# Applying the chunk inverses once per unit instead of once per chunk in an RWKV-7 recurrence

## The chip, the cores and the metric

The kernel runs on one core of a Trainium2 chip. The metric is the device time of one execution in microseconds (us). Before the change the median of three timed runs is 1398.25 us (1395.99 to 1398.87).

TensorE (PE in the profile) multiplies and writes its results to PSUM, the accumulation memory; its weight loads are listed apart as PEld. VectorE (DVE), ScalarE (ACT) and GpSimd (POOL) work element by element, and SyncE (SP) issues most DMAs.

## The reference

One layer for a prompt of 1024 tokens and 8 samples of 4 tokens: an RWKV-7 recurrence beside dilated attention, then a gated merge, an output projection and a layer norm. The change touches the recurrence of the prompt, cut here to its core (per head, with a 64 x 64 state S):

```python
def step(S, inp):
    r_t, w_t, k_t, v_t, kk_t, a_t = inp
    sa = jnp.einsum('bhvk,bhk->bhv', S, -kk_t)
    S = (S * w_t[:, :, None, :] + sa[..., None] * (kk_t * a_t)[:, :, None, :]
         + v_t[..., None] * k_t[:, :, None, :])
    return S, jnp.einsum('bhvk,bhk->bhv', S, r_t)

S_fin, o = lax.scan(step, wkv0.astype(F32), xs)
```

Each token reads the state that all tokens before it have written, so the plain form has 1024 steps in a row.

## The kernel before

**Chunks.** The 1024 tokens are cut into 16 chunks of 64. Inside a chunk the tokens' effect on each other is a lower triangular matrix, and the corrections `sa` of all its tokens come from one triangular solve. Two heads (e = 0, 1) share the 128 partitions. A *unit* is a pair of heads and half of the sequence, so 8 chunks; there are 8 units (4 pairs, 2 halves), numbered 0 to 7 here.

**What a unit prepares** (`unit`, L304): the decays `E`, the tile `KR` with the kappa vectors in its middle columns and the receptance vectors in its outer ones, the tile `BK`, and `AT`, which is `BK` times `KR` per chunk and head (L369) under a mask (L376, VectorE). From `AT` and the values in `W` comes `R0`, the tokens' own part of the right-hand side (L415, copied by L419). The inverse of the triangular part is made by `inverse` (L425): 32 x 32 blocks go out to DRAM, 31 steps on VectorE (L440, L443) solve them, and they come back.

**What a unit's recurrence does** (`scan`, L454): first the blocks are joined to 64 x 64 inverses with two batches of small matmuls (L466, copied by L472, then L476, copied by L482 back into `AT`). Then for each chunk in turn:
- L495: `KR` of the chunk times the state. One half of the rows is kappa times the state, the other half the receptance times the state.
- L497 (VectorE): the first half plus `R0` gives `R`; L498 (ScalarE) copies the other half to the output tile `Ot`.
- L502: the chunk's inverse times `R`, two matmuls, one a head. L503 (ScalarE) copies it negated into `W`.
- L507: `BT` (the transposed `BK`) times `W` is the update; L510 (VectorE) adds it to the decayed state `SD`, which L493 (ScalarE) has scaled.

After the eighth chunk L518 makes the rest of the output in one batch, and `norm` (L527) normalises it (its transposes on TensorE are L547, copied by L549).

**What sets the order.** TensorE's order is written out by hand: `run_streams` (L700) keeps a clock, and each generator (recurrence, norms, inverses, preparations) yields how long its piece takes TensorE and after how long its next piece is due. Whoever is due goes first, the recurrence ahead of the others; when nobody is due, one piece of a projection follows (L171, a third of a bank's 12 matmuls, four matmuls). The projections are the input matrix's columns for the recurrence, its gates and the rest, and they fill the stage until none is left. ScalarE, VectorE and the DMA queues are ordered by the scheduler. PSUM is shared out by tags: projections "pj" (four banks), the recurrence "sc" (two), the preparations and norms "g" (two). A tile of a tag waits until an earlier one of that tag has been read. The tag "t" is a ring of six buffers in SBUF.

Of the kernel before, what the change touches and what calls it, by code (L numbers as in the profile page):

```python
# [14 lines left out]
AF = mybir.ActivationFunctionType  # L15
ALU = mybir.AluOpType
AX = mybir.AxisListType

P = 128
# [13 lines left out]
D_PM, D_HOP, D_ST, D_GN, D_IN, D_WU = 0.53, 0.99, 1.54, 12.6, 11.0, 0.48  # L33
# [49 lines left out]
def tile_layer(ctx: ExitStack, tc: tile.TileContext, A: dict, O: list):  # L83
    nc = tc.nc
    V, S, G, T, SP = nc.vector, nc.scalar, nc.gpsimd, nc.tensor, nc.sync
# [10 lines left out]
    def mk(pool, shape, tag, bufs=None, dt=F32):  # L96
        uid[0] += 1
        return pool.tile(list(shape), dt, tag=tag, name=f"{tag}_{uid[0]}", bufs=bufs)

    def ps(tag, cols=512, parts=P):  # L100
        pool = pspool if tag == "pj" else pp[0]
        return mk(pool, [parts, cols], tag, {"pj": PJ, "sc": 2, "g": 6 - PJ, "s": 1, "t": 2, "o": 1}[tag])


    ident = mk(cpool, [P, P], "ident")[:]
# [9 lines left out]
    rp = rw_stack.enter_context(tc.tile_pool(name="rp", bufs=1))  # L115
# [94 lines left out]
    for c in range(3):  # L210
# [5 lines left out]
        if c == 2:  # L216
            prm = mk(cpool, [P, 57], "prm")
            b = ps("g")
# [10 lines left out]
    b = ps("g")  # L229
# [224 lines left out]
    def scan(j, hf, KR, AT, W, BT, R0, E, bon, st, Xd, blk, out):  # L454

        T1 = mk(rp, [P, 8, 32], "T1", 1)
        quads = [(p, 64 * (1 - p), n, n // 4, 2 * (n % 4) + p) for p in range(2) for n in range(8)]
        for p in range(2):
            u = 64 * (1 - p)
            for b in (1, 0):  # L460
                SP.dma_start(blk(p, b, slice(0, 2)), Xd[p, b].rearrange("e c j i -> j e c i"))
            V.transpose(T1[u : u + 32], AT[u : u + 32, :, p::2, u : u + 32])
        both = [quads[8 * p + n] for n in range(8) for p in range(2)]
        pm = ps("sc")
        for _, u, n, e, c in both:
            T.matmul(  # L466
                pm[u + 32 : u + 64, 32 * n : 32 * n + 32], AT[u : u + 32, e, c, u + 32 : u + 64], T1[u : u + 32, n, :],
                start=True, stop=True,
            )
        for p in range(2):  # L470
            u = 64 * (1 - p)
            S.activation(T1[u + 32 : u + 64], pm[u + 32 : u + 64, 0:256].rearrange("p (a b) -> p a b", a=8), AF.Copy, scale=-1.0)  # L472
        yield (0.5, D_PM)
        pg = ps("sc")
        for _, u, n, e, c in both:
            T.matmul(  # L476
                pg[u : u + 32, 32 * n : 32 * n + 32], T1[u + 32 : u + 64, n, :], AT[u + 32 : u + 64, e, c, u + 32 : u + 64],
                start=True, stop=True,
            )
        for p in range(2):  # L480
            u = 64 * (1 - p)
            S.activation(  # L482
                AT[u : u + 32, :, p::2, u + 32 : u + 64], pg[u : u + 32, 0:256].rearrange("p (a b c) -> p a b c", a=2, b=4), AF.Copy
            )
        yield (0.6, D_PM)

        Ot = mk(rp, [P, 4, P], "Ot", 2)
        for c in range(8):
            p, c2 = c % 2, c // 2
            u, v = slice(64 * (1 - p), 64 * (1 - p) + 64), slice(64 * p, 64 * p + 64)  # L490
            S0, S1 = st[c % 2], st[1 - c % 2]
            SD = mk(rp, [P, P], "SD", 1)
            S.activation(SD[:], S0[:], AF.Copy, scale=E[:, c, 64:65])  # L493
            pr = ps("sc")
            T.matmul(pr[:, 0:P], KR[:, c2, 2 * p : 2 * p + 2, :], S0[:], start=True, stop=True)  # L495
            R = mk(rp, [P, P], "R", 1)
            V.tensor_tensor(R[u], pr[u, 0:P], R0[u, c2, :], ALU.add)  # L497
            S.activation(Ot[v, c2, :], pr[v, 0:P], AF.Copy)  # L498
            yield (0.2, D_HOP)
            pu = ps("sc")  # L500
            for e in range(2):
                T.matmul(pu[u, 64 * e : 64 * e + 64], AT[u, e, c, u], R[u, 64 * e : 64 * e + 64], start=True, stop=True)  # L502
            S.activation(W[u, c, :], pu[u, 0:P], AF.Copy, scale=-1.0)  # L503
            yield 0.4, D_WU

            pS = ps("sc")
            T.matmul(pS[:, 0:P], BT[:, c, :], W[:, c, :], start=True, stop=True)  # L507
            for e in range(2):
                d = slice(64 * e, 64 * e + 64)
                V.scalar_tensor_tensor(S1[d, d], pS[d, d], E[d, c, 64:65], SD[d, d], ALU.mult, ALU.add)  # L510
            yield (0.2, D_ST)


        po = ps("g")
        for c in range(8):
            c2, v = c // 2, slice(64 * (c % 2), 64 * (c % 2) + 64)
            for e in range(2):
                T.matmul(  # L518
                    po[v, c2 * P + 64 * e : c2 * P + 64 * e + 64], AT[:, e, c, v], W[:, c, 64 * e : 64 * e + 64],
                    start=True, stop=True,  # L520
                )
        V.tensor_tensor(Ot[:], Ot[:], po.rearrange("p (a b) -> p a b", a=4), ALU.add)
        yield (2.0, 0.0)
        out.append((j, hf, Ot, bon))
# [156 lines left out]
    def scans():  # L681
        for u in range(8):
            while done["inv"] <= u or done["unit"] <= u:
                yield None
            args = ready[u]
            yield from scan(*args, *inv[u], looped)
            if args[1]:
                state_out(args[0], args[9])
                yield 0.1, 0.0
            done["scan"] += 1  # L690
# [59 lines left out]
    def rec_step(t, w):  # L750
        Ss, kv, vv, oo = (rec[n] for n in ("S", "kv", "vv", "oo"))
        part = slice(8 * w, 8 * w + 8)
        R = Ss[:, part, :]
        bc = lambda i: kv[:, t, i, :].unsqueeze(1).to_broadcast([P, 8, 64])
# [4 lines left out]
        sa = mk(sp, [P, 8], "sa", 2)  # L759
        yield V.tensor_tensor(tm[:], R, bc(1), ALU.mult)  # L760
        yield V.tensor_reduce(sa[:], tm[:], AX.X, ALU.add)
        yield V.tensor_tensor(R, R, bc(0), ALU.mult)
        yield V.tensor_tensor(tm[:], vb(sa[:]), bc(2), ALU.mult)
        yield V.tensor_tensor(R, R, tm[:], ALU.subtract)
        yield V.tensor_tensor(R, R, kvp[:], ALU.add)  # L765
# [429 lines left out]
    for h in range(4):  # L1195
# [5 lines left out]
        for g in range(3):  # L1201
# [11 lines left out]
            a, b_ = attend(h, g, z["q"], z["k"], z["v"], ml, os_), s_scores(h, g, Sa, sm)  # L1213
# [136 lines left out]
```

## Time and profile before

| | |
|---|---|
| median of the timed runs | 1398.25 us |
| the profiled execution, in all | 1401.51 us |
| its span on the core | 1399.7 us |
| mean granted TensorE clock | 0.992 of full speed |
| first and last L495 (state product of a chunk) | 151.0 and 596.4 us |
| last L518 (rest of the output) | 602.3 us |
| costliest line, L171 (projections) | three rows of 401.6, 382.9 and 384.4 us |

The page lists for each engine the busy time and its share of the span. In a row on a line of the kernel stand the line, the engine, the operation, the tiles written and read with their shapes, then the busy time, the mean of one in ns, and the idle time of the engine ahead of it with what ended it. TensorE runs a 32-bit matmul as two records, so L502's 128 instructions are 256 rows. A matmul's end is modelled and overlaps the next one's start.

### The profile page before, as it was taken

To read this page: it belongs to the slowest core of one execution; us is meant where nothing else is said; L and a number is where in the kernel's file an instruction comes from. 1 tells how busy PE (TensorE), PEld (TensorE's weight loads), DVE (VectorE), ACT (ScalarE), POOL (GpSimd) and SP (SyncE) were. 2 spreads that over 40 slices of the span, in tenths; PEclk is the share of its full clock that TensorE was granted. 3 is DMA by queue.
4 is the path that set the end of the run, shared out by engine and by line. 5 is a ranking of instruction groups with operands and counts; after the bars stand their busy time and mean duration, and the time that the engine had idled before them with its cause. 6 is when DMAs were issued, how large, how long until landed. Compare 5 with 4: busy or idle time off the path is not lost.

```text
span 1399.7 us, 25258 instructions
## 1 busy us (share of the span) xinstructions
PE 1354.1 (97%) x9765; PEld 1250.6 (89%) x9765; DVE 814.9 (58%) x2219; ACT 460.6 (33%) x1075; POOL 81.2 (6%) x92
## 2 busy tenths in 40 slices
PE   7999999999999999998999999999999999999997
PEld 7998988898888889998999889989998899898884
DVE  4358767587776767343655485547233524565675
ACT  4333444444344443321332323322323234132110
POOL 0000000000000000001000000000000000025122
PEclk9999999999999999999999999999999999999999
DMA  6112222312313233237545454545565556687121
GB/s 213 54 46 74 60 78 80 97 50 73 88 51 89 77 89 101 81 96 141 102 106 117 113 128 101 123 116 133 97 151 122 122 128 153 173 252 243 61 90 53
DMA packets 339743, 151.29 MB, mean 108 GB/s; under 512 B 188945, under 2 KB 329031, under 8 KB 339367
## 3 DMA queue, kind: packets, MB, share of 16 engines
q1 hardware_dynamic: 249190, 133.55, 35.1%
q10 hardware_dynamic: 90432, 16.13, 6.3%
q8 instruction: 77, 1.26, 0.4%
q14 instruction: 44, 0.35, 0.1%
HBM read 110.35 MB, written 38.97 MB: 107 GB/s over the span
## 4 chain that ended last, share of the span: by engine, by line
PE 74%; DVE 13%; DMA 7%; issue 2%; ACT 2%; SPq 1%; POOL 1%; DVEq 0%; ACTq 0%
PE pj L171 51%; PE pj L1310 7%; PE o L931 2%; PE s L894 2%; DVE X L443 2%; DVE tm L440 2%; DMA cb<-cd 2%; DMA gt<-gd 1%; PE t L914 1%; DMA kv<-vd 1%; PE sc L502 1%; PE s L1013 1%; PE g L369 1%; DVE wlo L162 1%; DVE st L510 1%
## 5 line engine op out<-in xcount | busy, mean ns | idle before, releaser
L171 PE MATMUL pj<-xhi,whi 128*128 128x352 f32 x1848 | 401.6, 338 | 4.8 <-ACT whi L161 3.7
L171 PE MATMUL pj<-xhi,wlo 128*128 128x352 f32 x1848 | 382.9, 329 | 4.7 <-DVE wlo L162 4.7
L171 PE MATMUL pj<-xlo,whi 128*128 128x352 f32 x1848 | 384.4, 329 | 0.0
L171 PEld LDWEIGHTS pj<-xhi,whi 128*128 128x128 f32 x1848 | 304.5, 190 | 21.7 <-issue 10.4
L171 PEld LDWEIGHTS pj<-xhi,wlo 128*128 128x128 f32 x1848 | 309.0, 190 | 8.1 <-DVE wlo L162 5.3
L171 PEld LDWEIGHTS pj<-xlo,whi 128*128 128x128 f32 x1848 | 308.7, 190 | 2.9 <-issue 0.6
L162 DVE TENSOR_TENSOR wlo<-wraw,whi 128x512 fp32r<-128x512 f32 x162 | 111.6, 690 | 83.2 <-ACT whi L161 82.4
L161 ACT ACTIVATE whi<-wraw 128x512 fp32r<-128x512 f32 x162 | 100.8, 626 | 128.3 <-PE pj L171 79.1
L904 ACT ACTIVATE Sm<-Sm,nm 128x128 f32<-128x128 f32 (+1 forms) x96 | 42.4, 443 | 70.5 <-DVE nm L901 70.5
L510 DVE SCALAR_TENSOR_TENSOR st<-sc,E,SD 64x64 f32<-64x64 f32 x128 | 36.2, 283 | 47.0 <-PE sc L507 45.5
L1310 PE MATMUL pj<-wl,mh 128*128 128x512 f32 (+1 forms) x144 | 56.8, 394 | 0.0
L440 DVE TENSOR_TENSOR tm<-Y,X 128x60 f32<-128x60 f32 (+24 forms) x248 | 52.6, 212 | 6.3
L443 DVE TENSOR_TENSOR X<-X,tm 128x60 f32<-128x60 f32 (+24 forms) x248 | 52.0, 210 | 6.4
L896 DVE CUSTOM_DVE_ANT_0 Sm<-s,cst 128x128 f32<-128x128 f32 (+1 forms) x96 | 29.6, 346 | 40.4 <-PE s L894 40.4
L493 ACT ACTIVATE SD<-st,E 128x128 f32<-128x128 f32 x64 | 25.7, 401 | 58.5 <-DVE st L510 58.5
L819 ACT ACTIVATE k<-pj 128x352 f32<-128x352 f32 (+1 forms) x36 | 16.3, 456 | 84.9 <-PE pj L171 79.9
L757 POOL TENSOR_TENSOR kvp<-vv,kv 128x512 f32<-128x512 f32 x16 | 20.0, 1252 | 353.0 <-DVE Ss L765 226.7
L819 ACT ACTIVATE q<-pj 128x352 f32<-128x352 f32 (+1 forms) x36 | 16.4, 456 | 70.5 <-PE pj L171 68.3
L931 PE MATMUL o<-PT,Vt 128*128 128x128 f32 x280 | 38.5, 275 | 0.0
L894 PE MATMUL s<-k,q 128*128 128x128 f32 (+1 forms) x192 | 37.6, 325 | 0.0
L931 PEld LDWEIGHTS o<-PT,Vt 128*128 128x128 f32 x280 | 36.5, 191 | 0.6 <-ACT o L936 0.4
L819 ACT ACTIVATE v<-pj 128x352 f32<-128x352 f32 (+1 forms) x36 | 16.1, 451 | 61.3 <-PE pj L171 61.0
(295 smaller groups left out, 1756.2 us busy)
## 6 DMA issues: line engine op xcount, KB each, us to landing
wraw<-in_w_in_dram SPq DMA_DIRECT2D x146, 256.0 KB
gd<-zt SPq DMA_DIRECT2D x48, 176.0 KB
gt<-gd SPq DMA_DIRECT2D x48, 176.0 KB
vs<-bt ACTq DMA_DIRECT2D x48, 128.0 KB
kc<-in_cache_kv_g_dram SPq DMA_DIRECT2D x48, 128.0 KB
Vt<-vs ACTq DMA_DIRECT2D x12, 512.0 KB
cb<-cd SPq DMA_DIRECT2D x12, 512.0 KB
zd<-zt SPq DMA_DIRECT2D x24, 176.0 KB
```

Source lines behind the costliest of these rows:

```text
L161: S.activation(hi[:], raw[:], AF.Copy)
L162: V.tensor_tensor(lo[:], raw[:], hi.bitcast(F32)[:], ALU.subtract)
L171: T.matmul(out, w[wi][:, n % 4, :], x[:, n % 4, :], start=first and n == 0, stop=last and n == 11)
L440: V.tensor_tensor(tm, Y[:, r : r + 1, r + 1 : 32].to_broadcast([P, m, n]), X[:, 0:m, r : r + 1].to_broadcast([P, m, n]), ALU.mult)
L443: V.tensor_tensor(X[:, 0:m, r + 1 : 32], X[:, 0:m, r + 1 : 32], tm, ALU.subtract)
L510: V.scalar_tensor_tensor(S1[d, d], pS[d, d], E[d, c, 64:65], SD[d, d], ALU.mult, ALU.add)
L819: S.activation(classes(dst[:], d)[:, :, t0 // d : (t0 + n) // d], b[:, 0:n].rearrange("p (i c) -> p c i", c=d), AF.Copy)
L894: T.matmul(r, qT[:, i * P : (i + 1) * P], kT[:, keys[i][0] * P : keys[i][0] * P + n], start=True, stop=True)
L896: V.tensor_tensor_reduce(out=Sm[:, i, 0:n], in0=r, in1=m3 if g == 2 else m12[:, 256 - n : 256], scale=1.0, scalar=NEG, op0=ALU.add, op1=AL ...
L904: S.activation(Sm[:, i, 0:n], Sm[:, i, 0:n], AF.Exp, scale=SCALE, bias=nm[:, x : x + 1], accum_out=ml[:, g, 1, i : i + 1])
L931: T.matmul(po[:, (i % 4) * P : (i % 4 + 1) * P], st["Vt"][:, kb_, :], PT[:, n * P : (n + 1) * P], start=m == 0, stop=m == len(keys[i]) - 1,)
L1310: T.matmul(pb[0:n, :], a[:, k, 0:n], wk, start=x == 0, stop=x == len(prods) - 1)
```

## The change

Applying the inverse is linear, so it can be done to the two parts of the right-hand side apart: to the kappa vectors and to `R0`. Neither needs the state, so both are done ahead of the loop for all eight chunks of the unit:

- four transposes on TensorE turn the kappa part of `KR` (L467 in the changed kernel), and two ScalarE copies (L471) put it into a new tile `kT` of the ring "t";
- after the blocks are joined (now L474, L480, L484, L490), 16 matmuls of 64 x 64 multiply each chunk's inverse with its kappa (L500), into two "sc" banks, and ScalarE writes them negated over the kappa columns of `KR` (L505);
- 16 more (L510) multiply the inverses with `R0`, and ScalarE writes that negated over `R0` (L514).

In the loop the state product (L525) then gives the solved correction directly. VectorE adds `R0` into `W` (L526), and the update (L531, L534) follows. L502, L503 and the tile `R` are gone, as is their due time.

```diff
@@ scan @@
+        pk = ps("sc")
+        for c2 in range(4):
+            T.transpose(pk[:, c2 * P : (c2 + 1) * P], KR[:, c2, 1:3, :], ident)
+        kT = mk(rp, [P, 4, P], "t", 6)
+        for p in range(2):
+            u, v = slice(64 * (1 - p), 64 * (1 - p) + 64), slice(64 * p, 64 * p + 64)
+            S.activation(kT[u], pk[v, :].rearrange("p (a b) -> p a b", a=4), AF.Copy)
         pm = ps("sc")
         for _, u, n, e, c in both:
...
         yield (0.6, D_PM)
 
+        chunks = [(c // 2, c % 2, e) for c2 in range(4) for e in range(2) for c in (2 * c2, 2 * c2 + 1)]
+        pk = [ps("sc") for p in range(2)]
+        for c2, p, e in chunks:
+            u = slice(64 * (1 - p), 64 * (1 - p) + 64)
+            T.matmul(
+                pk[p][64 * e : 64 * e + 64, 64 * c2 : 64 * c2 + 64],
+                kT[u, c2, 64 * e : 64 * e + 64], AT[u, e, 2 * c2 + p, u], start=True, stop=True,
+            )
+        for p in range(2):
+            S.activation(KR[:, :, 1 + p, :], pk[p][:, 0:256].rearrange("p (a b) -> p a b", a=4), AF.Copy, scale=-1.0)
+        yield (1.3, 0.0)
+        pu = ps("sc")
+        for c2, p, e in chunks:
+            u = slice(64 * (1 - p), 64 * (1 - p) + 64)
+            T.matmul(
+                pu[u, c2 * P + 64 * e : c2 * P + 64 * e + 64],
+                AT[u, e, 2 * c2 + p, u], R0[u, c2, 64 * e : 64 * e + 64], start=True, stop=True,
+            )
+        S.activation(R0[:], pu.rearrange("p (a b) -> p a b", a=4), AF.Copy, scale=-1.0)
+        yield (1.3, D_PM)
+
         Ot = mk(rp, [P, 4, P], "Ot", 2)
         for c in range(8):
...
             T.matmul(pr[:, 0:P], KR[:, c2, 2 * p : 2 * p + 2, :], S0[:], start=True, stop=True)
-            R = mk(rp, [P, P], "R", 1)
-            V.tensor_tensor(R[u], pr[u, 0:P], R0[u, c2, :], ALU.add)
+            V.tensor_tensor(W[u, c, :], pr[u, 0:P], R0[u, c2, :], ALU.add)
             S.activation(Ot[v, c2, :], pr[v, 0:P], AF.Copy)
             yield (0.2, D_HOP)
-            pu = ps("sc")
-            for e in range(2):
-                T.matmul(pu[u, 64 * e : 64 * e + 64], AT[u, e, c, u], R[u, 64 * e : 64 * e + 64], start=True, stop=True)
-            S.activation(W[u, c, :], pu[u, 0:P], AF.Copy, scale=-1.0)
-            yield 0.4, D_WU
 
             pS = ps("sc")
             T.matmul(pS[:, 0:P], BT[:, c, :], W[:, c, :], start=True, stop=True)
```

Three places of the order show it. First TensorE in one chunk of the loop of unit 0, before (from the state product L495 to the next one; "pj" are projection banks, "sc" the recurrence's):

```order
L495 MATMUL sc_1719<-st_80_482,KR_885 128x128
L171 MATMUL pj_1583<-xlo_10_88,whi_1682 128x352 x4
L171 MATMUL pj_1584<-xhi_8_86,whi_1682 128x352 x4
L502 MATMUL sc_1736<-R_1721,AT_976 64x64 x2
L171 MATMUL pj_1584<-xhi_8_86,wlo_1683 128x352 x4
L507 MATMUL sc_1744<-W_1017,BT_1029 128x128
```

The same engine and place in the changed kernel, where the state product is L525 and the update L531:

```order
L525 MATMUL sc_1721<-st_79_481,KR_885 128x128
L171 MATMUL pj_1582<-xhi_8_86,whi_1727 128x352 x4
L171 MATMUL pj_1582<-xhi_8_86,wlo_1728 128x352 x4
L531 MATMUL sc_1739<-W_1017,BT_1029 128x128
L171 MATMUL pj_1582<-xlo_10_88,whi_1727 128x352 x4
L171 MATMUL pj_1583<-xhi_8_86,whi_1727 128x352 x4
L171 MATMUL pj_1583<-xhi_8_86,wlo_1728 128x352 x4
L525 MATMUL sc_1760<-st_80_482,KR_885 128x128
```

The two small matmuls and the group of projections behind them have left the chunk: it has five groups of projections where it had six.

Second, TensorE at the start of the recurrence of unit 1, before: the two joining batches (L466, L476), with the second half of the next unit's masked products (L369, eight matmuls into two "g" banks) between them, then the last unit's output transposes (L547):

```order
L466 MATMUL sc_2370<-T_425_2363,AT_1345 32x32 x16
L369 MATMUL g_2389<-KR_2276,BK_2285 128x128
L369 MATMUL g_2390<-KR_2276,BK_2285 128x128
...
L476 MATMUL sc_2401<-AT_1345,T_425_2363 32x32 x16
L547 MATMUL g_2420<-ident_69,Ot_1668 128x128 x4
L388 MATMUL g_2432<-t_2288,cst_76 128x512
L495 MATMUL sc_2438<-st_79_481,KR_1230 128x128
```

The same place on TensorE in the changed kernel:

```order
L467 MATMUL sc_2350<-ident_69,KR_1230 128x128 x4
L474 MATMUL sc_2358<-T_412_2343,AT_1345 32x32 x16
L571 MATMUL g_2377<-ident_69,Ot_1718 128x128 x4
L369 MATMUL g_2388<-KR_2244,BK_2253 128x128
L369 MATMUL g_2389<-KR_2244,BK_2253 128x128
...
L484 MATMUL sc_2400<-AT_1345,T_412_2343 32x32 x16
L388 MATMUL g_2420<-t_2256,cst_76 128x512
L500 MATMUL sc_2423<-AT_1345,t_2355 64x64
...
L510 MATMUL sc_2443<-R_264_1501,AT_1345 64x64 x16
```

The output transposes (now L571) have come ahead of the masked products and take one of the two "g" banks there. In units 3 and 5 it is the same; in units 2, 4 and 6 both masked products, L571 and the transposes of `BK` (L406) are ahead of L467, with one projection group between the joining batches; in units 0 and 7 there is only that group.

Third, ScalarE at the start of unit 1, before:

```order
L472 ACTIVATE T_425_2363<-sc_2370 32x256 x2
L482 ACTIVATE AT_1345<-sc_2401 32x8x32 x2
L549 ACTIVATE Ot_1668<-g_2420,prm_339 128x512
L399 ACTIVATE W_2443<-g_2444 64x4x128
L498 ACTIVATE Ot_2435<-sc_2438 64x128
```

And in the changed kernel, where L471 copies `kT` and L505 the kappa columns of `KR`:

```order
L471 ACTIVATE t_2355<-sc_2350 64x512 x2
L480 ACTIVATE T_412_2343<-sc_2358 32x256 x2
L573 ACTIVATE Ot_1718<-g_2377,prm_339 128x512
L309 ACTIVATE t_2586<-m_798,prm_339 128x512
L490 ACTIVATE AT_1345<-sc_2400 32x8x32 x2
L505 ACTIVATE KR_1230<-sc_2423 128x4x64
L505 ACTIVATE KR_1230<-sc_2424 128x4x64
L514 ACTIVATE R_264_1501<-sc_2443 128x512
```

The two copies of `kT` stand ahead of those of the first joining batch (T1, printed as `T`), and the output's copy L573 behind both, ahead of the copies into `AT`. In unit 0 the next unit's Square (L309) stands between the copies of `kT` and of T1.

## The prediction

> **What bounds the kernel now.** I read the page first, then the table by stage, then the chain, then single instructions in order of time.
>
> ```profile
> span 1399.7 us, 25258 instructions
> PE 1354.1 (97%) x9765; PEld 1250.6 (89%) x9765; DVE 814.9 (58%) x2219; ACT 460.6 (33%) x1075; POOL 81.2 (6%) x92
> ...
> 250.00:350.00 100.00, 97.21 (x852) 87.96 (x848) 74.35 (x256) 44.09 (x99) 0.32 (x2) 1.00 0.26 72
> 605.00:620.00 15.00, 15.00 (x96) 14.98 (x95) 8.51 (x23) 4.63 (x9) 0.00 (x0) 1.00 0.36 109
> ...
> 602.82 14.22 PE pj L171 x88
> 617.04 0.44 PE g L547 x4
> 617.48 7.12 PE pj L171 x44
> ```
>
> The rows with a colon give a stretch in us, then the busy time of PE, PEld, DVE, ACT and POOL. TensorE is the bound of the whole recurrence stage: 97 us of 100 in its middle, and no gap at its end. The chain rows show that at the end it isn't the recurrence that is late. The last chunk is over at 602.6 us, and 22 us of projections still follow. A shorter chain from chunk to chunk therefore buys nothing by itself. What counts is how long TensorE takes for its list, and how long it stands still between. So I price the change in TensorE's start-to-start times and waits, not in the latency of a chunk.
>
> **What a chunk pays now.** One chunk's TensorE rows (start, duration; durations overlap, so a cost is the distance to the next start):
>
> ```profile
> 164.98 0.81 PE L171 MATMUL pj<-xhi,wlo 128*128 128x352 f32 x4
> 165.63 0.38 PE L495 MATMUL sc<-st,KR 128*128 128x128 f32 x2
> 165.76 0.90 PE L171 MATMUL pj<-xlo,whi 128*128 128x352 f32 x4
> 166.50 0.80 PE L171 MATMUL pj<-xhi,whi 128*128 128x352 f32 x4
> 167.24 0.44 PE L502 MATMUL sc<-R,AT 64*64 64x64 f32 x4
> 167.61 0.91 PE L171 MATMUL pj<-xhi,wlo 128*128 128x352 f32 x4
> 168.35 0.38 PE L507 MATMUL sc<-W,BT 128*128 128x128 f32 x2
> 168.49 0.89 PE L171 MATMUL pj<-xlo,whi 128*128 128x352 f32 x4
> 169.22 0.81 PE L171 MATMUL pj<-xhi,whi 128*128 128x352 f32 x4
> 169.87 0.81 PE L171 MATMUL pj<-xhi,wlo 128*128 128x352 f32 x4
> 170.52 0.38 PE L495 MATMUL sc<-st,KR 128*128 128x128 f32 x2
> ```
>
> An undisturbed group of four projection matmuls takes 0.65 (164.98 to 165.63). The chunk takes 170.52 - 165.63 = 4.89, of which six such groups are 3.89; 1.00 is the recurrence. L495 and L507 cost 0.13 each and stretch the next group to 0.74, so 0.22 each. L502, which the change removes, takes 0.37 and stretches the group before it and the one behind it to 0.74: 0.55. Eight chunks in each of eight units: **64 x 0.55 = 35.2 us go.** The ScalarE copy L503 and the half of the chunk's VectorE work that stays (L497 now writes W) lie beside TensorE, so I cost them at nothing there; what waits on them is counted below.
>
> **What the batches add.** Per unit: 4 transposes of 128x128, and twice 16 matmuls of 64x64. The second kind stands in the trace already (L415, each instruction two records), the transposes as L396.
>
> ```profile
> 103.80 0.81 PE L171 MATMUL pj<-xhi,whi 128*128 128x352 f32 x4
> 104.54 1.15 PE L415 MATMUL g<-W,AT 64*64 64x64 f32 x32
> 105.62 0.92 PE L171 MATMUL pj<-xhi,wlo 128*128 128x352 f32 x4
> 106.38 0.95 PE L312 MATMUL g<-cst,t 128*128 128x2 f32 x8
> ...
> 447.37 0.66 PE L396 MATMUL g<-ident,m 128*128 128x128 f32 x4
> 447.78 0.89 PE L171 MATMUL pj<-xhi,wlo 128*128 128x352 f32 x4
> 448.06 1.20 ACT L399 ACTIVATE W<-g 64x512 f32<-64x512 f32 x2 [0.31 <-PE g L396]
> 449.31 0.66 PE L406 MATMUL g<-ident,BK 128*128 128x128 f32 x4 [0.42 <-ACT W L399]
> ```
>
> A batch of 16 takes 1.08, with 0.09 and 0.11 of stretching around it. Two in a row: 2 x 1.08 + 0.20 = 2.36. The transposes take 0.40. So 2.76 per unit, **22.1 us come.** The matmuls alone make 22.1 - 35.2 = -13.1 us.
>
> **The new waits.** All the added PSUM copies go to ScalarE, and all the added matmuls use the two "sc" buffers, in a stretch where the next step needs the one before at once. TensorE takes its list in order, so the projections stand behind each of these waits too. ScalarE's prices:
>
> ```profile
> 148.20 0.69 PE L466 MATMUL sc<-T,AT 32*32 32x32 f32 x32
> 148.82 0.92 PE L171 MATMUL pj<-xhi,whi 128*128 128x352 f32 x4
> 148.94 0.78 ACT L472 ACTIVATE T<-sc 32x256 f32<-32x256 f32 x2 [3.08 <-PE sc L466]
> 149.67 0.78 PE L476 MATMUL sc<-AT,T 32*32 32x32 f32 x32
> ...
> L549 ACT ACTIVATE Ot<-g,prm 128x512 f32<-128x512 f32 x8 | 6.1, 765 | 3.7 <-PE g L547 3.6
> L309 ACT ACTIVATE t<-m,prm 128x512 f32<-128x512 f32 x8 | 5.7, 713 | 0.8 <-DVE lst L261 0.8
> ```
>
> *The copies of T1 come behind those of kT.* The two kT copies have the shape of L399: they begin 0.69 after the transposes (447.37 to 448.06) and take 1.20. T1's two take 0.78 more. From the start of the transposes that is 2.7 us. (kT takes one of the six "t" buffers whose tile was read long before, and no step that moves issues a DMA.) TensorE wants the second block product (L476, now L484) after 0.40 + 0.62 + 0.74 = 1.76. In the five units with only a projection group between (0, 2, 4, 6, 7) it stands 0.94; a copy of BT is still running in three of them, so I take 1.0 us for each, and in unit 0 another 0.75, as the Square of the next unit (L309) has come between the copies. Now it stands 0.1 there, in units 0 and 7: +5.5.
>
> *A buffer of "g" hangs on the same queue.* In units 1, 3 and 5 the transposes of the last output (L547, now L571) come ahead of the second mask product, whose second matmul needs their buffer back. That copy (0.765) is behind kT's and T1's: 2.7 + 0.8 = 3.5, wanted at 1.6: 1.9 us. How long this place waits now:
>
> ```profile
> 203.69 0.69 PE L466 MATMUL sc<-T,AT 32*32 32x32 f32 x32
> 204.54 1.75 PE L369 MATMUL g<-KR,BK 64*128 64x128 f32 x16 [0.15 <-DVE AT L376]
> 206.13 1.29 DVE L376 TENSOR_TENSOR AT<-g,cst 128x512 f32<-128x512 f32 x2 [1.04 <-PE g L369]
> 206.22 0.69 PE L476 MATMUL sc<-AT,T 32*32 32x32 f32 x32
> 206.87 0.66 PE L547 MATMUL g<-ident,Ot 128*128 128x128 f32 x4
> ...
> L502 PE MATMUL sc<-R,AT 64*64 64x64 f32 x256 | 28.2, 230 | 2.6 <-DVE R L497 2.3
> L507 PE MATMUL sc<-W,BT 128*128 128x128 f32 x128 | 25.4, 279 | 0.6 <-ACT W L503 0.4
> L406 PE MATMUL g<-ident,BK 128*128 128x128 f32 x64 | 10.0, 279 | 2.6 <-ACT W L399 2.6
> ```
>
> L466 takes 0.62 where it doesn't wait, so the mask product is late by 0.23 at its start; the 1.68 to the next row against 1.08 for as many records is 0.6 more: 0.83 now. So +1.1 in each of three units: +3.3. In units 2, 4 and 6 the output's transposes follow that product at once, and the masks (206.13 to 207.42) hold them where L476 covered 0.65: +0.6 each, with what is late behind: +1.8.
>
> *The second batch reuses the buffer of the first.* L510 waits until the first kappa copy has read it. No row shows a 128x256 copy; by its free size the nearest is L472 (0.39 each), and bounds are nothing (another buffer free) and 0.7 (like L309). After L415's kind of batch the results are there 1.15 from its start, the copy ends near 1.55, and 1.08 was wanted: 0.45 in all eight units, +3.6 (0 to 6.4). L500 itself waits for the AT copies only where little lies between, units 0 and 7: +0.7.
>
> *Waits that go.* L406 no longer waits for L399, since the buffers fall differently: -2.6. The wait of L507 for the copy of W goes: 0.6 on the row, and groups behind it are stretched too: -1.0. The 2.6 of L502 for R stays, on the state product: it has the same two groups of cover, and the same VectorE queue ahead of it, so I move it whole.
>
> New waits: 5.5 + 3.3 + 1.8 + 3.6 + 0.7 - 2.6 - 1.0 = **+11.3 us**. Sum: -13.1 + 11.3 = -1.8. Behind the last chunk the same projections stand without a gap, so all of it reaches the end. From the span, 1399.7 to 1397.9; the profiled execution took 1401.5 in all, 3.3 above the median of the timed runs, and I carry the difference over to that median: 1398.25 - 1.8 = **1396.4 us**. A measurement of this kernel can tell about 0.2%, 2.8 us, from no change.
>
> **Rivals.** *Faster: the waits don't come together.* If ScalarE is ahead, or TensorE's other groups happen to lie between, at worst all of 14.9 us of new waits falls away: -16.7, 1381.5. For it speaks that ACT is 44% busy in the middle; against it that the copies follow from each other, not from ACT's load. Half of them gone gives -9.3, 1389. I give 0.36 to a gain over 2.8 us.
>
> *Slower: ScalarE is busy when the transposes end.* ACT takes its work in order. One weight split (L161) or projection copy in front shifts the T1 copies, and once more the AT copies ahead of L500:
>
> ```profile
> L161 ACT ACTIVATE whi<-wraw 128x512 fp32r<-128x512 f32 x162 | 100.8, 626 | 128.3 <-PE pj L171 79.1
> ```
>
> That is 0.63 once or twice in eight units, 5 to 10 us: +3.2 to +8.2, 1401.5 to 1406.5. The change loses from 16.7 / 8 = 2.1 us of new waits per unit on; I count 1.9. For it speaks that all new copies sit on the one queue; against it the 3.08 that ACT idled before L472 in unit 0. Chance 0.2. [...]
>
> *Slower by far: the batches don't stream.* At L502's 0.37 for two matmuls, 256 new ones would cost 47 in place of 17: +28, 1426. L415, of the same tile, speaks against it. 0.03.
>
> **How the numbers follow.** Within 0.2% has 0.41, faster 0.36, slower 0.23. The range from 1388 (rather more than half of the new waits gone) to 1403 (ScalarE one copy late in every unit) leaves out about 0.1 on each side.
>
> **What would show it.** L502's successor gone and a chunk with five projection groups in 3.7 us; L500 and L510 at 1.1 us each; waits of L484 for the T1 copies of about 1.0, of the second mask product for L573, of L510 for L505; the recurrence over about 30 us earlier (64 x 0.65 of projections moved behind it, less the new waits) with the stage's end hardly moved. If PE shows no idle at L484 and L510, the faster rival is right; if each unit's start has more than 2.1 us of new idle, the slower one.

## The result, and the profile after

The changed kernel takes 1418.0 us (median of 4 runs, 1412.5 to 1418.5) against 1398.6 of the kernel before: ratio 1.0114, 95% interval 1.0092 to 1.0136. It is slower by 1.1%, and the forecast of 1396.4 with its range up to 1403 did not hold it. The profiled execution took 1418.52 us; its span is 17.0 us longer than that of before.

The page of after: the span, the busy shares and the granted clock in 40 slices. Then the clock over the whole span, of after and of before:

```profile
span 1416.7 us, 25818 instructions
PE 1360.0 (96%) x10053; PEld 1259.6 (89%) x10053; DVE 812.4 (57%) x2219; ACT 463.9 (33%) x1051; POOL 81.2 (6%) x92
...
PEclk9999898999998999999999999999999999999999
```

```profile
core 0: 1416.7 us, clock 0.982
```

```profile
core 0: 1399.7 us, clock 0.992
```

Before, every slice of the clock's row shows a 9. After, three slices in the recurrence stage show 8. The table by stage (the clock is the third column from the end):

```profile
150.00:250.00 100.00, 94.43 (x794) 87.10 (x795) 66.22 (x246) 41.35 (x92) 0.32 (x2) 0.90 0.20 57
250.00:350.00 100.00, 94.70 (x928) 85.32 (x927) 69.79 (x233) 44.26 (x94) 0.43 (x3) 0.98 0.28 73
350.00:450.00 100.00, 94.94 (x815) 87.38 (x814) 78.65 (x284) 40.15 (x87) 2.11 (x7) 0.98 0.26 71
450.00:550.00 100.00, 93.18 (x861) 83.51 (x854) 65.88 (x242) 42.34 (x98) 3.93 (x8) 0.95 0.27 77
```

TensorE is less busy than before (94.7 in place of 97.2 in the second row), and its clock is below full: 10 + 2 + 2 + 5 = 19 us of full-speed time are missing. In the traces of before and after the record of the clock (10 and 20 entries) has only two values, 1.0 and 0.5, and in each it changes on one grid of 3.413 us: every entry but the last is a whole multiple of that long. After has 11 half-clock stretches of 3.413 us between 150 and 605 us, before none. Half of a stretch is 1.71 us; that is what it would take from TensorE, with work throughout, if every start-to-start time doubled. In after a group of four projections takes 1.17 us in such a stretch (171.19 to 172.36 us) and 0.65 at full clock (165.30 to 165.95), so by my estimate a stretch full of them costs 3.413 x (1 - 0.65 / 1.17) = 1.5 us more than at full clock.

What goes ahead of such a stretch is seen at the start of unit 1. First its rows in order of time, then the windows of the grid:

```profile
206.22 0.60 PE L467 MATMUL sc<-ident,KR 128*128 128x128 f32 x4
206.75 0.69 PE L474 MATMUL sc<-T,AT 32*32 32x32 f32 x32
207.19 1.19 ACT L471 ACTIVATE t<-sc 64x512 f32<-64x512 f32 x2 [2.07 <-DVE AT L376]
...
208.39 0.76 ACT L480 ACTIVATE T<-sc 32x256 f32<-32x256 f32 x2
209.18 0.78 ACT L573 ACTIVATE Ot<-g,prm 128x512 f32<-128x512 f32 x1
...
210.01 1.16 PE L369 MATMUL g<-KR,BK 64*128 64x128 f32 x14 [1.56 <-ACT Ot L573]
```

```profile
207.63:211.05 3.42, 1.86 (x20) 1.42 (x18) 1.03 (x2) 2.88 (x6) 0.00 (x0) 1.00 0.16 47
211.05:214.46 3.41, 3.41 (x48) 1.80 (x50) 1.82 (x4) 0.75 (x2) 0.00 (x0) 0.50 0.29 91
214.46:217.87 3.41, 2.92 (x64) 2.62 (x58) 0.43 (x1) 0.80 (x3) 0.00 (x0) 0.50 0.29 55
217.87:221.29 3.42, 3.42 (x16) 3.42 (x16) 0.29 (x1) 1.98 (x5) 0.00 (x0) 0.50 0.03 12
221.29:224.70 3.41, 3.41 (x25) 3.41 (x25) 0.85 (x3) 2.04 (x5) 0.00 (x0) 1.00 0.28 94
```

The copies of `kT`, of T1 and of the last output stand in line on ScalarE, and the mask product waits 1.56 us for the third; the forecast had this place, with 1.9 us. In that window TensorE is busy for 1.86 of 3.42 us. The next three windows run at half clock: 10.2 us, which cost up to 5.1 us more than at full clock. None of this was in the sum. Nine of the 11 stretches come behind the starts of units 0, 1, 3 and 5. The other two (from 170.09 and 422.67 us) follow waits of the preparation (L293) for VectorE, of 0.65 and 1.24 us.

The waits themselves, from 140 to 640 us (last columns: idle time ahead of the row, and what ended it), after and then before:

```profile
L531 PE MATMUL sc<-W,BT 128*128 128x128 f32 x128 | 27.7, 298 | 3.9 <-DVE W L526 3.7
L525 PE MATMUL sc<-st,KR 128*128 128x128 f32 x128 | 26.7, 291 | 2.2 <-DVE st L534 2.1
L369 PE MATMUL g<-KR,BK 64*128 64x128 f32 x192 | 17.0, 289 | 5.7 <-ACT Ot L573 4.3 <-DVE AT L376 1.1
L510 PE MATMUL sc<-R,AT 64*64 64x64 f32 x256 | 11.7, 257 | 3.9 <-ACT KR L505 3.9
L484 PE MATMUL sc<-AT,T 32*32 32x32 f32 x256 | 7.5, 204 | 2.8 <-ACT T L480 2.8
L293 PE MATMUL g<-lorh,lhi 64*128 64x512 f32 (+1 forms) x20 | 7.0, 403 | 2.7 <-DVE nt L316 2.6
L571 PE MATMUL g<-ident,Ot 128*128 128x128 f32 x32 | 5.2, 285 | 1.7 <-DVE AT L376 1.7
```

```profile
L369 PE MATMUL g<-KR,BK 64*128 64x128 f32 x192 | 16.8, 288 | 2.1 <-DVE AT L376 1.5
L293 PE MATMUL g<-lorh,lhi 64*128 64x512 f32 (+1 forms) x20 | 6.0, 404 | 0.7 <-DVE nt L316 0.7
L547 PE MATMUL g<-ident,Ot 128*128 128x128 f32 x32 | 5.1, 283 | 0.2 <-DVE AT L376 0.2
```

### The profile page after: what moved, and what is told of

It is laid out like the page before. It is cut to its first block, busy times and chain, and to the rows that moved or that the text cites. A ratio compares the mean times of both kernels' runs of the same rounds, so it can differ in the third digit from the quotient of the medians.

```text
span 1416.7 us, 25818 instructions
## 1 busy us (share of the span) xinstructions
PE 1360.0 (96%) x10053; PEld 1259.6 (89%) x10053; DVE 812.4 (57%) x2219; ACT 463.9 (33%) x1051; POOL 81.2 (6%) x92
## 4 chain that ended last, share of the span: by engine, by line
PE 70%; DVE 16%; DMA 7%; ACT 3%; issue 2%; SPq 1%; POOL 0%; ACTq 0%; DVEq 0%
PE pj L171 47%; PE pj L1334 7%; PE s L918 2%; PE o L955 2%; DVE tm L440 2%; DVE X L443 2%; DMA cb<-cd 2%; DVE wlo L162 1%; PE t L938 1%; DVE st L534 1%; DMA kv<-vd 1%; PE s L1037 1%; DMA wraw<-in_w_in_dram 1%; PE sc L510 1%; PE sc L531 1%
## 5 line engine op out<-in xcount | busy, mean ns | idle before, releaser
L526 DVE TENSOR_TENSOR W<-sc,R 64x128 f32<-64x128 f32 x64 | 18.4, 287 | 56.6 <-PE sc L525 55.6
L534 DVE SCALAR_TENSOR_TENSOR st<-sc,E,SD 64x64 f32<-64x64 f32 x128 | 36.1, 282 | 23.6 <-PE sc L531 21.8
L843 ACT ACTIVATE k<-pj 128x352 f32<-128x352 f32 (+1 forms) x36 | 16.3, 455 | 83.6 <-PE pj L171 74.9
L257 DVE SCALAR_TENSOR_TENSOR m<-pj,prm,m 128x351 f32<-128x351 f32 (+1 forms) x39 | 22.3, 571 | 32.1 <-ACT m L256 31.8
```

The costliest lines, as they stand in the source:

```text
L843: S.activation(classes(dst[:], d)[:, :, t0 // d : (t0 + n) // d], b[:, 0:n].rearrange("p (i c) -> p c i", c=d), AF.Copy)
```

## The experiments

In after the six windows at full clock that stand ahead of the half-clock stretches were idle for 0.65, 0.98, 1.24, 1.28, 1.42 and 1.56 us. **Theory 1**, an estimate from these: a window of 3.41 us in which TensorE stands idle for about a third is followed by one at half clock; the new waits, most of them at the units' starts, bring this about, and it is most of the loss. **Theory 2:** the loss is the waits and mispriced work; the clock is a side show. **Theory 3:** runs of small matmuls (32 x 32, 64 x 64) count as idle for the clock, waits or not. All ratios below are to the kernel before on the same chip (1401 to 1402 us there).

### Covering the waits

e1 raises the due times behind L474, L484 and L500, so that more work that doesn't depend on them stands ahead of each step: up to three groups of projections from behind the recurrence, or pieces of the preparation.

```diff
-        yield (0.5, D_PM)
+        yield (0.5, 1.2)
-        yield (0.6, D_PM)
+        yield (0.6, 1.2)
-        yield (1.3, 0.0)
+        yield (1.3, 1.2)
```

> The changed kernel with three due times raised (0.53, 0.53 and 0.0 to 1.2), so that about two projection groups stand behind the second transposing batch, the kappa batch's inputs and the kappa batch; no work is added or left out. Theory 1 (clock: a 3.41 us window in which TensorE idles for about a third or more is followed by 3.41 us at half clock, 1.7 us lost): the waits of L484, L500 and L510 (8 us in all) go, and unit 0 with its two slow stretches; units 1, 3 and 5, whose mask product waits for L573, keep at least one each: 1402 to 1409 us, granted clock 0.986 to 0.990. Theory 2 (the loss is the idle time itself and work under-priced, the clock follows by itself): only the 6 to 8 us go, 1410 to 1412, clock 0.982 as before. Theory 3 (runs of 32x32 and 64x64 matmuls count as idle for the clock): the clock stays at 0.982 or below, 1410 or above.

> The changed kernel with the three due times at 1.2, again, on the chip of the other three: ratio 0.994 to 0.998, clock 0.991 to 0.994 in its runs.

Measured: 1395.1 us, ratio 0.9964 (0.9941 to 0.9987), clock 0.993 in the profile; on another chip 0.9963 (0.9947 to 0.9979). The same batches and products, and it is faster than the kernel before. Its rows for the places above:

```profile
L369 PE MATMUL g<-KR,BK 64*128 64x128 f32 x192 | 16.7, 288 | 2.4 <-DVE AT L376 1.6 <-ACT Ot L573 0.4
L510 PE MATMUL sc<-R,AT 64*64 64x64 f32 x256 | 9.2, 221 | 0.0
L484 PE MATMUL sc<-AT,T 32*32 32x32 f32 x256 | 6.0, 192 | 0.2 <-ACT T L480 0.2
```

L510 and L484 wait for next to nothing. The norm's copy stands elsewhere too, so units 1, 3 and 5 got more relief than theory 1 had allowed for. Theory 3 as it stands, that the batches lower the clock whether TensorE waits or not, falls: all batches are there, and the clock is that of before. As e1 also puts more work between the batches, it doesn't tell whether small matmuls add to a wait; the windows further below do. Theory 2's 1410 falls too.

e1 also gives a ledger, since it has as many half-clock stretches in the stage as before (3 each, the stage's ends included; after has 13). TensorE's start-to-start times less idle time, from the 301st projection matmul to attention's first product, worked out from the three traces, in us:

```
                          before    after      e1
projections L171           455.3    456.2   451.1
L502 / L467, L500, L510     24.0     22.2    17.6
state product and update    21.8     24.6    23.8
all other rows              93.0     98.9    92.6
idle                        15.2     27.8    20.2
sum                        609.3    629.7   605.3
```

Without idle time: before 594.1, after 601.9, e1 585.1. At equal clock the change saves 9.0 us of work; the half clock puts 16.8 back on (10 stretches at 1.5 to 1.71 make 15 to 17.1); the waits add 12.6. Together +20.4 at the stage's end; with the rest of the execution it is +17.0. The 16.8 can be checked from the record of the clock: in this part TensorE was busy at half clock for 42.6 us in after and for 10.2 in e1, and half of the difference, the most that full clock would have saved, is 16.2.

As a control e5 gives the kernel before the same larger due times behind its own two batches.

```diff
-        yield (0.5, D_PM)
+        yield (0.5, 1.2)
-        yield (0.6, D_PM)
+        yield (0.6, 1.2)
```

> The kernel before, with the two due times that it shares with the changed one (behind L466 and L476) raised from 0.53 to 1.2; no work is added or left out. It is the control for the changed kernel with raised due times, which ran 0.36% under the kernel before. If that gain is the change's own (the added and removed products, with the clock out of the way), this kernel stays at the kernel before, ratio 0.998 to 1.002; if it came from the due times, this one gains as much, ratio 0.996.

Measured 1.0044 (1.0025 to 1.0062): slower, outside both forecasts. The gain of e1 is not the due times' own.

### Waits alone, in the kernel before

e3 puts a wait into the loop of before, far from the batches; e4 has four copies in place of two, and e11 two of e3's waits per place, with `yield (0.5, 0.53)` behind each:

```diff
         for c in range(8):
...
+            if c in (2, 6):
+                pz = ps("sc")
+                for q in range(2):
+                    T.transpose(pz[:, q * P : (q + 1) * P], ident, ident)
+                zz = mk(rp, [P, 256], "zz", 1)
+                for q in range(2):
+                    S.activation(zz[:], pz[:, 0:256], AF.Copy)
+                py = ps("sc")
+                T.transpose(py[:, 0:P], zz[:, 0:P], ident)
```

> The kernel before, with a wait of TensorE put ahead of the state product in chunks 2 and 6 of each of the 8 units (16 places, all far from the start of a unit, no batch beside them): two transposes, two ScalarE copies of 128x256 one behind the other, and one transpose that waits for them. Own work of TensorE 16 x 0.3 = 5 us, idle 16 x about 1.0 = 16 us. Theory 1: an idle of 1.0 is about the bound for a window of 3.41 us, so 0 to 5 slow stretches more than before, 1418 to 1428, clock 0.987 to 0.992. Theory 2 and theory 3: no slow stretch beyond the one of before, 1418 to 1420, clock 0.992.

> As the short wait, with four copies one behind the other: idle 16 x about 1.8 = 29 us, own work 5 us. Theory 1: most of the 16 waits leave over a third of some window idle, 11 to 16 slow stretches of 3.41 us, 19 to 27 us of clock on top: 1450 to 1460, clock 0.974 to 0.980. Theory 2 and theory 3: the waits cost their own length, 1430 to 1434, and the clock stays at 0.992.

> The kernel before with two of the short waits (about 1.0 us idle each, two copies) at each of the 16 places, with one or a few projection groups between the two, in place of one wait. Own work of TensorE 16 x 2 x 0.48 = 15 us, idle 16 x 2 x 1.0 = 33 us. If what counts is the sum of idle time in a 3.41 us window, pairs that stand one group apart act like one wait of 2 us (which brought 17 stretches at 16 places): 8 to 16 added half-clock stretches, 14 to 27 us: 1463 to 1476, clock 0.976 to 0.984. If only a single idle gap counts, and 1.0 us is too short for it (three stretches at 16 places): 3 to 6 added stretches, 1454 to 1460, clock 0.988 to 0.991.

The row of the waiting transpose, of e3 and of e4:

```profile
L500 PE MATMUL sc<-ident,zz 128*128 128x128 f32 x16 | 5.3, 329 | 16.3 <-ACT zz L498 16.3
```

```profile
L500 PE MATMUL sc<-ident,zz 128*128 128x128 f32 x16 | 5.7, 356 | 31.5 <-ACT zz L498 31.5
```

Waits of 16.3/16 = 1.02 us brought 4 half-clock stretches into the stage and 1425.7 us (clock 0.991); waits of 1.97 us brought 16, and 1454.0 us (clock 0.977). That is as theory 1 had it, and without any part of the change. The 28.3 us between the two are less than the 15.2 us of longer waits and 12 stretches at 1.71 make. In the ledger's way of counting, over the same part, e4 has 12.2 us more idle time than e3 (other waits shrank by 3) and 17.6 us more of the rest, for 13 more stretches: 1.35 each. Why it is less than the 1.5 of a stretch full of projections isn't shown; TensorE was busy in 57 of the 58 us of e4's stretches there. A window of e4 with a wait of 2.0 us in it, and the next one:

```profile
249.21:252.62 3.41, 1.42 (x10) 1.17 (x8) 3.04 (x14) 2.46 (x6) 0.00 (x0) 1.00 0.00 0
252.62:256.03 3.41, 3.37 (x13) 2.99 (x14) 0.70 (x4) 0.28 (x1) 0.00 (x0) 0.50 0.48 109
```

e11 took 1458.1 us at a clock of 0.988. That is the forecast for the case that only a single gap counts; its 7 stretches in the stage lie between the two cases. But few pairs fell into one window. In three windows the waits made 1.84 to 1.99 us together, no single one being over 1.44, and each was followed by half clock, so there the sum counted. Two rows of waits and their window:

```profile
226.48 0.33 PE L501 MATMUL sc<-ident,zz 128*128 128x128 f32 x1 [1.04 <-ACT zz L499]
...
228.62 0.47 PE L501 MATMUL sc<-ident,zz 128*128 128x128 f32 x1 [0.95 <-ACT zz L499]
```

```profile
225.25:228.66 3.41, 1.42 (x10) 0.97 (x8) 0.44 (x1) 1.91 (x6) 0.00 (x0) 1.00 0.64 181
228.66:232.08 3.42, 3.42 (x14) 3.42 (x15) 0.29 (x1) 0.77 (x2) 0.00 (x0) 0.50 0.42 102
```

All windows at full clock between 140 and 650 us of the 18 profiled executions, by TensorE's idle time in them:

```
idle in the window   windows   next one at half clock
under 0.6 us            2457     3
0.6 to 1.2 us            120    17
1.2 to 1.8 us             32    18
over 1.8 us               11    11
```

The windows also differ by what TensorE does between the waits. The same ones, parted by whether smaller matmuls than 128*128 in the rows (the batches, the mask products, some of the preparation) take more than 0.12 us of them:

```
                     128*128 alone        with smaller ones
idle in the window   windows   next half  windows   next half
under 1.2 us            1312     0           1265    20
1.2 to 1.8 us             12     0             20    18
over 1.8 us                9     9              2     2
```

With 128*128 matmuls alone none of the 1324 windows idle for up to 1.72 us was followed by half clock, and all 9 from 1.84 us on were: half of the window, not a third. With smaller ones beside, 20 of the 22 from 1.2 us on were. The table fits a weaker form of theory 3 beside theory 1, in which time in small matmuls adds to the idle time. No run varied this alone, so whether and how much a small matmul counts stays open.

### Which waits

e2 copies `kT` on VectorE; e8 raises the third due time alone; e6 is the kernel before with the transposes and copies of `kT` alone, read by nobody; e14 is the changed kernel with only the preparation's due times raised (behind L312 and the mask products).

```diff
e2   -            S.activation(kT[u], ..., AF.Copy)
     +            V.tensor_copy(kT[u], ...)
e6   +        pk = ps("sc")
     +        ... (the lines of L467 to L471)
e8   -        yield (1.3, 0.0)
     +        yield (1.3, 1.2)
e14  -        yield (0.4, 0.0)
     +        yield (0.4, 1.2)
     -            yield (1.7, D_G)
     +            yield (1.7, 1.2)
```

> The changed kernel with the two copies of the transposed kappa (L471) on VectorE instead of ScalarE. The copies of T1 (L480) and the norm's L573 then no longer stand behind 1.2 us of L471. Theory 1: units 1, 3 and 5 lose 1.2 us of their 1.6 us wait and with it most of their seven slow stretches, units 0, 2, 4, 6 and 7 about 0.8 us of L484's wait each: 3 to 5 us of waits and 10 to 15 us of clock, 1398 to 1405 us at a clock of 0.988 to 0.992. Theory 2: only the waits, 1410 to 1414. Theory 3: clock 0.982 as it was, 1410 to 1414.

> The changed kernel with the third due time alone raised (0.0 to 1.2), so that groups stand between the kappa batch and the batch that waits for its copies. L510's waits (8 x 0.5 = 4 us) go. Theory 1: they went along with the other waits in units 0, 1, 3 and 5, whose windows stay idle by L573 and L480 alone: of the 11 added half-clock stretches 3 to 6 go, 5 to 10 us: 1403 to 1410, clock 0.984 to 0.987. Theory 2: 4 us, 1414 to 1416.

> The kernel before with one part of the change alone: the four transposes of kappa (L467) and their two ScalarE copies, whose result nobody reads; the loop and its inverse per chunk are those of before. Own work of TensorE 8 x 0.53 = 4 us. Theory 1: the copies of T1 and, in units 1, 3 and 5, the norm's copy stand behind the added copies, and TensorE waits for them, about 8 x 0.8 + 3 x 1.5 = 11 us; half-clock stretches follow in units 1, 3 and 5, 4 to 8 of them, 7 to 14 us: ratio 1.013 to 1.020, clock 0.984 to 0.989. Theory 2: the work and the waits alone, ratio 1.010 to 1.012, clock 0.992. Theory 3 (runs of small matmuls lower the clock): no batch is added, so the clock stays at 0.992.

> The changed kernel with the two due times of the preparation alone raised; its three batches' due times stay as the change has them. It tells whether the batches' own waits (L484, L510, 7 us in all) suffice for the lost clock without the preparation's waits beside them. Theory 1, sum of idle time per window: the waits for the norm's L573 and for L480 stay in place, 4 to 9 added half-clock stretches: ratio 1.002 to 1.008, clock 0.984 to 0.988. If the preparation's waits were what tipped the windows, at most 2 stretches: ratio 0.995 to 0.999, clock 0.991 or more.

- e2: 1406.4 us, 1.0036 (1.0016 to 1.0056), 7 half-clock stretches in the stage in place of 11. That is a little above theory 1's range; VectorE's own products came later (L474 now waited 1.8 us for T1).
- e8: 1406.0 us, 1.0033 (1.0021 to 1.0046), 3 stretches. More than L510's waits went: the last output's transposes now come behind L484 in units 1, 3 and 5, and most of the waits for L573 (4.3 us in after) went as well.
- e14: 1404.7 us, 1.0024 (1.0003 to 1.0045). Its profiled execution has 3 stretches, but it was one of the fastest, at 1400.2 of 1399.9 to 1412.2 us, and the waits for L573 (4.6) and of L510 (3.8) are still in it.

Two rows of e8:

```profile
L369 PE MATMUL g<-KR,BK 64*128 64x128 f32 x192 | 16.8, 293 | 1.5 <-DVE AT L376 0.6 <-ACT Ot L573 0.5
L510 PE MATMUL sc<-R,AT 64*64 64x64 f32 x256 | 9.2, 221 | 0.0
```

Each of the three takes other waits away, and each takes 11 to 13 us off the 1417.2 that the changed kernel took beside e1's repetition. That fits windows that are tipped by the sum of their waits. As each edit also shifts what stands near it, the share of a single wait stays open.

e6 missed: 1403.8 us, 1.0018 (1.0005 to 1.0030), one stretch. The waits that I had expected, 1.5 us at the masks (L369) in each of three units and 0.8 us ahead of the second joining batch (here L483) in each of eight, are hardly there:

```profile
L369 PE MATMUL g<-KR,BK 64*128 64x128 f32 x192 | 15.9, 287 | 0.1
L483 PE MATMUL sc<-AT,T 32*32 32x32 f32 x256 | 7.0, 193 | 1.6 <-ACT T L479 1.5
```

In the order of before the output's transposes come behind that batch, so nothing that TensorE wants soon stands behind the `kT` copies. The wait for L573 takes the copies and the changed order together. As the waits didn't come, e6 tells nothing of the clock.

### The change as it is, again

> The changed kernel itself, on the same chip. Theory 1: where the windows of 3.41 us fall differs from execution to execution, so the runs spread with their clock: each 0.001 of the mean clock (of about 1415 us) is 2 x 1.4 = 2.8 us of half clock and costs 1.4 us; from 0.981 to 0.989 the times fall by about 11 us. Median 1412 to 1420, ratio 1.008 to 1.014. Theory 2: no such relation, the times spread as those of the kernel before at one clock.

Ratio 1.0112 (1.0084 to 1.0141). The ten runs of the changed kernel, by mean clock and time:

```
0.979 1424.9   0.981 1418.3   0.981 1419.1   0.982 1417.7   0.982 1418.5
0.984 1417.5   0.986 1413.3   0.987 1417.0   0.988 1413.4   0.989 1412.5
```

Their slope is 0.94 us per 0.001; 85 runs of the kernel before beside these experiments have 1.14 (0.988 to 0.996). Both are below the 1.4 of e12's estimate, in which half clock doubles every time, and both are there, so the relation speaks for theory 1 with a smaller price. The profiled executions of the changed kernel and of its reorderings (after, e12, e1, e10, e2, e8) say the same: counted as in the ledger, the work without idle time rises by 0.98 us for each us that half clock takes from a busy TensorE (six executions, up to 2.7 us off the line). At 0.993, about where the kernel before runs, the line gives 1408.7 (it leaves the range of the runs there): some 7 us of the loss would stay, what the waits cost beyond the saved work (3.6 us by the ledger).

### What is best

e7 puts three groups in place of two between a chunk's two products (D_HOP 0.99 to 1.6) into e1. e9 and e16, one kernel, add to e1 the preparation's two due times of e14. e15 has all of these. e13 is the kernel before with the preparation's two.

```diff
-D_PM, D_HOP, D_ST, D_GN, D_IN, D_WU = 0.53, 0.99, 1.54, 12.6, 11.0, 0.48
+D_PM, D_HOP, D_ST, D_GN, D_IN, D_WU = 0.53, 1.6, 1.54, 12.6, 11.0, 0.48
```

> The changed kernel with the three due times at 1.2, and with three projection groups instead of two between a chunk's two products (D_HOP from 0.99 to 1.6). L531 waited 6 us in all for VectorE's W. If such waits are what is left, they fall to 1 or 2 us, and the time by 4 to 6 us to 1388 to 1392 on a chip where the kernel before takes 1401, clock 0.992 to 0.995; the last chunk moves by 64 x 0.65 = 42 us to about 632, still ahead of the last projections. If VectorE itself is what is late (its queue, not the distance), the wait moves to the next product and the time stays at 1395.

> The changed kernel with the three due times at 1.2 and two more of the preparation's raised to 1.2 (behind L312, whose bank the second lora product takes over, and behind each half of the mask products). In the kernel with three, TensorE still waited 1.8 us for the first, 4.3 us for the masks and the norm's transposes. If the distance is what lacks, these 6 us go to about 2 and no half-clock stretch is left in the stage but the one of before: 1389 to 1393 where the kernel before takes 1401, ratio 0.991 to 0.995. If VectorE's queue is what is late, the waits turn up elsewhere, as with three groups between a chunk's products, and the ratio stays at 0.996 to 0.999.

> The kernel before with the two due times of the preparation raised to 1.2, which both kernels share; those behind its own batches stay at 0.53, since raising them made it slower. Control for the fastest kernel so far (the changed one with five raised due times, 0.9906 of the kernel before). If the gain of 0.94% is the change's, this one stays at 0.997 to 1.002. If the preparation's due times give their part to any version, it falls by the half-clock stretch and the 1.3 us wait ahead of unit 0 and a few waits, 3 to 5 us: ratio 0.996 to 0.998, and the change's own part is 0.5%, 7 us.

> The changed kernel with all five due times at 1.2 and three groups between a chunk's two products. In the kernel with five, 7.6 us of waits of L531 for VectorE's W are the largest that is left. If distance covers them now that the preparation's products stand further apart, 4 to 6 us go: ratio 0.986 to 0.989. If VectorE's queue is late, the waits move to L525 as they did with three due times raised, and the ratio stays at 0.990 to 0.994.

> The changed kernel with five due times at 1.2, again, on the chip of the control: ratio 0.988 to 0.993, clock 0.993 to 0.995 in its runs.

e7: 0.9987 (0.9971 to 1.0004), rather slower than e1; the waits went from L531 (6.2 us in e1, 0.4 here) to L525 (2.2, now 6.1) and L293 (1.8, now 4.6), nearly all of them for VectorE, so its queue was late. e9: 1388.5 us, 0.9906 (0.9887 to 0.9926); e16 0.9916 (0.9898 to 0.9933). The control e13: 0.9974 (0.9960 to 0.9987), so a quarter to a third of that gain is open to the kernel before as well. e15: **1385.0 us, 0.9871** (0.9855 to 0.9886), the fastest, with no half-clock stretch between 140 and 640 us. Its rows:

```profile
L525 PE MATMUL sc<-st,KR 128*128 128x128 f32 x128 | 26.4, 288 | 7.0 <-DVE st L534 6.2 <-ACT t L336 0.4
L531 PE MATMUL sc<-W,BT 128*128 128x128 f32 x128 | 25.4, 280 | 0.3 <-DVE W L526 0.3
```

Here too the wait moved on to L525, against my expectation for a gain, and the time fell all the same. Where that gain comes from the runs don't settle. A kernel before with three groups between its products wasn't tried, nor one with all of its raised due times at once, nor a PSUM bank of its own for L510.

## Why the prediction was wrong

**What bounds the kernel: right.** TensorE's list and its waits set the end. The last chunk's output (L542) starts at 607.3 us where L518 stood at 601.4, and projections run on behind it.

**The removed and added work: sign right, too large.** A chunk with five groups takes 3.67 us where no wait stands, forecast as 3.7:

```profile
592.57 0.38 PE L525 MATMUL sc<-st,KR 128*128 128x128 f32 x2
592.71 0.89 PE L171 MATMUL pj<-xhi,wlo 128*128 128x352 f32 x4
593.43 0.81 PE L171 MATMUL pj<-xlo,whi 128*128 128x352 f32 x4
594.08 0.38 PE L531 MATMUL sc<-W,BT 128*128 128x128 f32 x2
...
596.24 0.38 PE L525 MATMUL sc<-st,KR 128*128 128x128 f32 x2
```

L502's own 24.0 us went, and the batches cost 17.6 where I had 20.5 without their stretching: by e1's rows L500 takes 0.62, L510 the 1.08 forecast, the transposes 0.53 in place of 0.40:

```profile
148.17 0.60 PE L467 MATMUL sc<-ident,KR 128*128 128x128 f32 x4
148.70 0.69 PE L474 MATMUL sc<-T,AT 32*32 32x32 f32 x32
...
154.22 0.69 PE L500 MATMUL sc<-AT,t 64*64 64x64 f32 x32
154.84 0.91 PE L171 MATMUL pj<-xhi,whi 128*128 128x352 f32 x4
...
156.97 1.15 PE L510 MATMUL sc<-R,AT 64*64 64x64 f32 x32
158.05 0.91 PE L171 MATMUL pj<-xhi,whi 128*128 128x352 f32 x4
```

The stretching of the projections gave back only 4.2, where 9.6 net were forecast, and the loop's two products rose by 2.0. At equal clock -9.0 in place of -13.1.

**The waits: places right, sum nearly.** +12.6 us in the ledger, +11.3 forecast. L484 stands 2.8 where 5.75 were forecast; the masks add 3.6 (3.3), the output's transposes 1.5 (1.8), L510 3.9 (3.6). Missed: L525 for the state, 2.2, and L293 for VectorE, 2.0 more than before. The 2.6 of L502 for R, which the prediction moved to the state product, stand as 3.9 at the update L531, the product that reads what VectorE now writes. Less the waits that went, there are 12.6 / 8 = 1.6 us of new waits per unit. By the forecast work the change loses from 13.1 / 8 = 1.6 on (the rival's 2.1 counts without the waits that go), by the measured work from 9.0 / 8 = 1.1. With both sizes put right its own steps give -9.0 + 12.6 = +3.6 at the stage's end, not +20.4. That would be about 1402 us, still inside its range.

**The step that failed** is the sentence that priced the change "in TensorE's start-to-start times and waits": every duration came from a trace at full clock, a wait was worth its own length, and a wait's effect on the clock of the work behind it was no term of the sum. That term came to 16.8 us in the ledger. No window of after was idle for more than 1.56 us, and in the second table of windows half clock followed such short idle times only where small matmuls stood beside them; the sum had priced those by their time alone. Covering the waits (e1), and making waits where the change isn't (e4), show it from both sides. The rival with ScalarE busy named the place and the queue, and its price of 3 to 8 us lacked the same term. The recurrence was not 30 us earlier either: waits and half clock had used it up.

## What to carry to other kernels

In this kernel, where TensorE was the bound, a wait cost its length and at times the speed of what followed. With 128*128 matmuls alone all 9 windows of 3.41 us idle for over 1.8 us were followed by half clock and none of 1324 idle for less; with small matmuls beside, 20 of 22 idle for over 1.2 us were. A stretch at half clock added 1.35 us (e4) to 1.68 (the ledger, 16.8 / 10). So add up the idle time per window, not per wait. When work is batched into a chain of small steps at one place, put independent matmuls between the steps from the start (0.9964 of the kernel before in e1, 1.0114 without), and look at the granted clock before looking for lost time in the rows. A change that loses may still be the better one: here the same products, given other due times, went from 1.1% slower to 1.3% faster than the kernel before with its own, which was not given all of them.

## What was not expected of the hardware

The clock fell after windows that were idle for only 1.2 to 1.8 of 3.41 us in 18 of 32 cases, all of them with small matmuls in the window, and in all 11 over 1.8. In unit 1 (above) three stretches followed one wait of 1.56 us, though TensorE was busy throughout the first of them, with small matmuls (L484 and L500) for 1.4 us of it. And two batches of 16 matmuls of 64 x 64 differ in price: in e1 L500, whose 16 use all four combinations of row and column half, takes 0.62 us, L510 with two of the four 1.08. Whether the combinations are the cause was not tried alone.
